# A hybrid RWKV-7 / gMLP layer in one launch: split weights kept two pieces ahead through the last product, with a fourth buffer, and its operand loads issued by ScalarE

## The chip, the cores and the metric

The kernel runs on one core of one Trainium2 chip. The metric is the device time of one execution in microseconds. The time before is the median of three runs, 3248.74 us (3248.45 to 3251.41). A separate execution of the same program was recorded by the hardware profiler; all traces below come from it.

## What is computed

One inference step of one layer, on 512 latent tokens and 128 context tokens (T = 640) of width 2048, all in float32. The reference, cut to the layer:

```python
h = _rmsnorm(x, lp['norm1_g']) * (1.0 + sc1) + sh1
p = h @ lp['w_in']
o_a, s_fin = _rwkv7_bidir(shift_fn(p[..., :C_SHIFT], lp['mu_shift']), s0, lp)
o_b = _chunk_gmlp(jax.nn.gelu(p[..., C_SHIFT:]), lp)
x = x + g1 * (jnp.concatenate([o_a, o_b], axis=-1) @ lp['w_out'])
h = _rmsnorm(x, lp['norm2_g']) * (1.0 + sc2) + sh2
ff = (jax.nn.silu(h @ lp['w_ffn_gate']) * (h @ lp['w_ffn_up'])) @ lp['w_ffn_down']
return x + g2 * ff, s_fin
```

A last RMS norm follows. The part of interest is the last product, with w_ffn_down: 5632 hidden values to 2048 columns.

## The kernel before

**One float32 product as three.** TensorE works on a rounded format (the type fp32r in the profile). A float32 matrix is split into a high part (a rounding copy) and a low part (what the copy left out), and a product is the sum of high x high, high x low and low x high: three matmuls for each block of 128 hidden values (a k-block), at L1817, L1818 and L1819. Weights are split when they arrive, by `parts`: ScalarE copies the high part (L1635), VectorE subtracts the low part (L1636). Each pair hi, lo takes a buffer until its matmuls are done.

**Seven products instead of eight.** The product is cut into two halves of tokens (320 each), two of columns and two of hidden values, and `seven` makes it with seven block products instead of eight, in the order PORD = 1, 2, 3, 7, 5, 6, 4. Each product multiplies one piece of weights: a loaded block (b11, b21, b22), or a difference that GpSimd (POOL) makes from them (`combined`, L1730; the tile t3 and the overwritten blocks b12, b22, b21; a difference shows as `t<-rawd` or `rawd<-rawd`). The activations must be in seven corresponding forms. In the gate phase before, the forms 3, 5 and 4 are split and stored as ready halves in d_os; 1, 2, 7 and 6 are stored whole in d_op.

**The last phase.** The 22 pairs of hidden blocks are cut into six chunks c of 3, 3, 4, 4, 4 and 4 k-blocks (CHK), and each chunk walks over eight column pairs n: 48 steps, seven products each. A product is 9 matmuls of 128x320 in the first two chunks, 12 in the others. A step's results are added to `acc` in SBUF (L2034, L2036, L2038); the first chunk writes it. In the last step of a chunk (a turn) the results stay in PSUM banks for the next chunk's first step. In the last chunk the banks start with acc (`filled`, ScalarE copies at L2116), and each step ends with row work: residual, transposes back to tokens on TensorE (L2097), copies and sums of squares on ScalarE (L2098, L2101).

**What sets the order.** In `seven` the program splits one piece ahead of the product that runs: `ready` holds as many pieces at the start as b11 has blocks, in this phase one, and each product appends the next. The splits of a step begin in that step. A scheduler then places the instructions of each engine in an order of its own; TensorE's stays the program's. `parts` takes its buffers from `st`, three of them; in the gate phase each fourth split uses a buffer of the pool `gu`, which `gus` names. Before the last phase `gus` is emptied and `gu` is closed, so there are three.

**Operands of a chunk.** While a turn runs, `load_ops` fetches the next chunk's operands: `direct` loads the split forms from d_os into their place (`xd`, L1856); `load` fetches the whole forms from d_op into four rotating buffers (`opd`, L1862), and `part` splits them: ScalarE casts (L1869), VectorE subtracts (L1870), GpSimd for some k. All these loads, the weights' (L1841), and the gate phase's stores to d_os (L1940) are issued by SyncE (SP) in one order, and an issue waits in that queue until its buffer is free.

**At the border into the phase.** The last gate block's product 4 is added (L1974), passed through silu (L1975), multiplied (L1976); GpSimd makes its sums (L1919, L1921, L1924); `part` splits and stores them: cast `sp` on ScalarE (L1937), subtraction (L1938), stores (L1940). Then the pool `dn` is opened on the closed pools' space.

Of the kernel before, what the change touches and what calls it, by code (L numbers as in the profile page):

```python
# [54 lines left out]
CHK = (3, 3, 4, 4, 4, 4)  # L55
# [263 lines left out]
def flow_step(ctx: ExitStack, tc, x_prompt, x_sample, state_rwkv, c, c_ctx, w_mod, b_mod,  # L319
# [3 lines left out]
    nc = tc.nc  # L323
# [23 lines left out]
    for h in range(2):  # L347
        s = slice(CH * h, CH * h + CH)
# [29 lines left out]
    d_op = dp.tile([NFF // 2, 7, P, HALF], F32, name="d_op")  # L378
# [10 lines left out]
    st = ctx.enter_context(tc.tile_pool(name="st", bufs=3, side="right"))  # L389
# [754 lines left out]
    parts, praw = {}, []  # L1144
# [150 lines left out]
    with ExitStack() as ph:  # L1295
# [17 lines left out]
        for k in (1, 3):  # L1313
            s = slice(32 * k, 32 * k + 32)
# [265 lines left out]
    def xpool(i, j):  # L1580
        return xep if i < 3 and j < 4 else xcp if j < 4 else xdp
# [33 lines left out]
    PW, READY, gus = [], [], []  # L1615
# [13 lines left out]
    turn4 = itertools.cycle(range(4))  # L1629

    def parts(raw, nk=4):
        pool, kw = (gus[0], dict(bufs=1)) if gus and next(turn4) == 3 else (st, {})
        hi = pool.tile([P, 4, P], F32R, tag="hi", name="hi", **kw)
        lo = pool.tile([P, 4, P], F32R, tag="lo", name="lo", **kw)
        S.copy(hi[:, 0:nk], raw[:, 0:nk])  # L1635
        V.tensor_sub(lo[:, 0:nk], raw[:, 0:nk], hi[:, 0:nk].bitcast(F32))  # L1636
        return hi, lo

    with ExitStack() as ph:
# [21 lines left out]
        for hf in range(2):  # L1661
            s = slice(HALF * hf, HALF * hf + HALF)
            for m in range(KB):
                pool = pbig if m % 2 == 0 else pb2
# [20 lines left out]
        for _ in range(2):  # L1685
            READY.append(parts(PW.pop(0)))
# [36 lines left out]
    def tick():  # L1723

        while len(hooks) > lag[0]:
            hooks.pop(0)()

    def combined(out, a, b, nk=4):
        for o, p, q in zip(out, a, b):
            G.tensor_tensor(out=o[:, 0:nk], in0=p[:, 0:nk], in1=q[:, 0:nk], op=ALU.subtract)  # L1730
# [61 lines left out]
    def fresh(i):  # L1792

        return pP.tile([P, 512], F32, tag="P", name=f"P{i}")[:, 0:HALF], False

    def seven(b11, b12, b21, b22, x, hook, nk=4, bank=fresh, last=True):

        def combine(out, a, b):
            combined(out, a, b, nk)
        t3 = [st.tile([P, 4, P], F32, tag="raw", name="t3", bufs=3) for _ in b11]  # L1800
        combine(t3, b22, b12)
        combine(b12, b12, b11)
        src = {1: b11, 2: b21, 3: b22, 7: t3, 5: b12, 6: b22, 4: b21}
        order = [raw for i in PORD for raw in src[i]]

        ready = [parts(order.pop(0), nk) for _ in range(len(b11))]
        for o, i in enumerate(PORD):
            ps, filled = bank(i)
            nq = len(b11)
            for q in range(nq):  # L1810
                hi, lo = ready.pop(0)
                if order:
                    ready.append(parts(order.pop(0), nk))
                for k in range(nk):
                    xk = x(i, 4 * q + k)
                    f, l = q == 0 and k == 0 and not filled, q == nq - 1 and k == nk - 1 and last
                    TE.matmul(ps, hi[:, k, :], xk[:, 0, :], start=f, stop=False)  # L1817
                    TE.matmul(ps, hi[:, k, :], xk[:, 1, :], start=False, stop=False)  # L1818
                    TE.matmul(ps, lo[:, k, :], xk[:, 0, :], start=False, stop=l)  # L1819
            if i == 3:  # L1820
                combine(b22, b22, b12)
                combine(b21, b21, b22)
            if last:
                hooks.append(lambda o=o, ps=ps: hook(o, ps))
            tick()
            yield o
# [3 lines left out]
    starts = [sum(CHK[:c]) for c in range(len(CHK))]  # L1830

    steps = [(c, n) for c in range(len(CHK)) for n in (range(8) if c % 2 == 0 else range(7, -1, -1))]
    WD, XD = {}, {}

    def load_down(s):
        if s < len(steps):
            c, n = steps[s]
            for b, r, m in (("11", 0, 0), ("21", 1, 0), ("22", 1, 1), ("12", 0, 1)):
                raw = xap.tile([P, 4, P], F32, tag=next(wtags), name="rawd")
                r0 = (starts[c] + r * NFF // 2) * P  # L1840
                nc.sync.dma_start(raw[:, 0:CHK[c], :], w_ffn_down[  # L1841
                    0, r0:r0 + CHK[c] * P, (2 * n + m) * P:(2 * n + m + 1) * P].rearrange("(k p) n -> p k n", p=P))
                WD[s, b] = raw
                yield
# [3 lines left out]
    def load_ops(c):  # L1848

        got = {}  # L1850
        new = lambda i, k: xpool(i, k).tile([P, 2, HALF], F32R, tag=f"xo{i}_{k}", name="xd")

        def direct(i):
            for k in range(CHK[c]):
                XD[i, k] = x = new(i, k)
                nc.sync.dma_start(x.bitcast(F32), d_os[starts[c] + k, SPLIT.index(i)])  # L1856

        def load(i):
            for k in range(0, CHK[c], 2):
                n = min(2, CHK[c] - k)  # L1860
                t = xap.tile([P, 2, HALF], F32, tag=next(stags), name="opd")
                nc.sync.dma_start(t[:, 0:n, :], d_op[starts[c] + k:starts[c] + k + n, i - 1].rearrange("k p t -> p k t"))  # L1862
                got.setdefault(i, []).append((k, n, t))

        def part(i):
            for k, n, t in got[i]:
                for q in range(n):
                    XD[i, k + q] = x = new(i, k + q)
                    S.copy(x[:, 0, :], t[:, q, :])  # L1869
                    (G if (k + q) in POOLK else V).tensor_tensor(out=x[:, 1, :], in0=t[:, q, :],  # L1870
                                                               in1=x[:, 0, :].bitcast(F32), op=ALU.subtract)
        load(1)
        load(2)
        yield
        part(1)
        load(7)
        yield
        part(2)
        direct(3)
        load(6)  # L1880
        yield
        part(7)
        yield
        direct(5)
        part(6)
        yield
        direct(4)
        yield
# [96 lines left out]
    for f in range(2, NFF):  # L1985
        b = {n: [WB.pop((f, n, q)) for q in range(2)] for n in ("11", "12", "21", "22")}
# [24 lines left out]


    dn = ctx.enter_context(tc.tile_pool(name="dn", bufs=1))
    acc = dn.tile([P, 8, 7 * HALF], F32, name="acc")
    sse = dn.tile([P, NT, 8], F32, name="sse")
    slot = lambda n, i: acc[:, n, (i - 1) * HALF:i * HALF]
# [25 lines left out]
    def load_x1(n):  # L2042
        if n >= 0:
            xqs[n] = [xap.tile([P, T], F32, tag=f"x1_{(1, 9)[m]}", name="x1d") for m in range(2)]
            for m in range(2):
                nc.sync.dma_start(xqs[n][m], d_x1[2 * n + m])
# [62 lines left out]
    def filled(n, i):  # L2109
        k = fill.index((n, i))  # L2110
        for m, j in fill[k:k + 2]:
            if (m, j) not in banks:
                banks[m, j] = ps = fresh(j)[0]
                x = XD[1, 0][:, 0, :]
                TE.matmul(ps, x[:, 0:P], x, start=True, stop=False)
                S.copy(ps, slot(m, j))  # L2116
        return banks[n, i], True

    held = {}
    for s, (c, n) in enumerate(steps):  # L2120
        b11, b21, b22, b12 = ([WD.pop((s, b))] for b in ("11", "21", "22", "12"))
        dloads = itertools.chain(dloads, load_down(s + 2))
        final, turn, after = c == NC - 1, s % 8 == 7 and c < NC - 1, s % 8 == 0 and c > 0
        if final or turn and c == NC - 2:
            bank = lambda i, n=n: filled(n, i)
        elif after:
            bank = lambda i: (held[i], True)
        elif turn:
            def bank(i):
                held[i], _ = fresh(i)  # L2130
                return held[i], False
        else:
            bank = fresh
        if c >= NC - 2 and (final or turn):
            lag[0] = LAST_LAG
        for o in seven(b11, b12, b21, b22, lambda i, k: XD[i, k], None if turn else Last(n) if final else Sum(n),
                       CHK[c], bank, not turn):
            if turn:
                if o == 1:
                    ops = load_ops(c + 1)  # L2140
                    next(ops)
                if o in AT:
                    next(ops)
            elif s % 8 == 0 and o in BT:
                next(ops)
            if o > 2:
                next(dloads, None)
            if final and after and o == 2:
                load_x1(n)
            while later and o >= later[0][0]:  # L2150
                later.pop(0)[1]()
            if s == len(steps) - 1 and o == 5:
                while hooks:
                    hooks.pop(0)()
# [52 lines left out]
```

## Time and profile before

| | us |
|---|---|
| median of three runs | 3248.74 |
| profiled execution | 3247.45 |
| its span, from first to last instruction | 3244.2 |
| TensorE matmuls busy | 3107.5 |
| VectorE busy | 2333.3 |
| ScalarE busy | 1446.0 |
| GpSimd busy | 1260.9 |

The granted TensorE clock of the execution was 0.983 on average. In the rows of the profile PE is TensorE, PEld its weight loads, DVE VectorE, ACT ScalarE, POOL GpSimd, SP SyncE; a q behind a name is the engine's sequencer, which issues the DMAs. A row of a timeline gives start, length, engine, line, operation, output and inputs by their names in the program, and in brackets the idle time ahead and what ended it. A row of the waits names an engine and line, what it waited for, and total us, count and longest. A matmul's length overlaps the next one's; what counts is the distance from start to start.

### The profile page before, as it was taken

The page shows a single profiled execution, that of the slowest core. Times are in us where ns is not written, and L with a number is a line of the kernel's source. Part 1 is how long each engine was busy: PE and PEld are TensorE (multiplying, and loading weights), DVE is VectorE, ACT ScalarE, POOL GpSimd, SP SyncE. Part 2 cuts the span into 40 slices and gives each one's busy share as a digit, 9 for nine tenths or more (in the row PEclk, how much of TensorE's full clock was granted, in tenths as well). Part 3 has the DMA queues.
Part 4 walks back from the last instruction along what each step waited for, and adds up shares of the span by engine and source line. Part 5 has one row for each costly group of instructions (what it writes and reads, how often), then busy time and mean ns, then how long its engine had stood idle before and what let it go on. Part 6 is the DMA issues. An engine that isn't in the chain of part 4 may idle for free. (4 is left out here: it accounts for less than half of the span.)

```text
span 3244.2 us, 73519 instructions
## 1 busy us (share of the span) xinstructions
PE 3107.5 (96%) x28828; PEld 2877.5 (89%) x28828; DVE 2333.3 (72%) x4073; ACT 1446.0 (45%) x3161; POOL 1260.9 (39%) x1082
## 2 busy tenths in 40 slices
PE   5899999999998999898999999999999999999996
PEld 3698888889886877788999999999999999999986
DVE  4456767767666666547977877877877777777787
ACT  3244554555543333345644444444444444444365
POOL 0001222222220122301365666566666645555543
PEclk8899999999997999999999999999999999999998
DMA  8768788887896777455434434434433354554353
GB/s 319 254 183 237 212 224 212 237 233 192 230 233 191 215 222 226 136 152 175 123 108 130 125 105 128 127 107 123 123 116 118 110 180 151 160 160 141 110 170 119
DMA packets 741922, 553.00 MB, mean 170 GB/s; under 512 B 141688, under 2 KB 674184, under 8 KB 732744
## 3 DMA queue, kind: packets, MB, share of 16 engines
q1 hardware_dynamic: 729256, 534.62, 55.5%
q0 software_dynamic: 9984, 13.13, 1.7%
q8 instruction: 226, 3.70, 0.5%
q14 instruction: 120, 0.98, 0.1%
q10 hardware_dynamic: 2336, 0.57, 0.1%
HBM read 438.77 MB, written 111.69 MB: 170 GB/s over the span
## 5 line engine op out<-in xcount | busy, mean ns | idle before, releaser
L1819 PE MATMUL P<-xo,lo 128*128 128x320 f32 x2352 | 727.1, 309 | 3.5 <-DVE lo L1636 3.5
L1818 PE MATMUL P<-xo,hi 128*128 128x320 f32 x2352 | 727.6, 309 | 0.0
L1817 PE MATMUL P<-xo,hi 128*128 128x320 f32 x2352 | 727.6, 309 | 0.0
L1636 DVE TENSOR_TENSOR lo<-raw,hi 128x512 fp32r<-128x512 f32 x532 | 514.4, 974 | 162.0 <-ACT hi L1635 159.6
L1635 ACT CAST hi<-raw 128x512 fp32r<-128x512 f32 x532 | 330.2, 622 | 505.6 <-PE P L1818 435.6
L1819 PEld LDWEIGHTS P<-xo,lo 128*128 128x128 f32 x2352 | 441.6, 188 | 4.3 <-DVE lo L1636 4.2
L1818 PEld LDWEIGHTS P<-xo,hi 128*128 128x128 f32 x2352 | 442.3, 188 | 0.0
L1817 PEld LDWEIGHTS P<-xo,hi 128*128 128x128 f32 x2352 | 442.3, 188 | 0.0
L1730 POOL TENSOR_TENSOR raw<-raw 128x512 f32<-128x512 f32 x252 | 413.6, 1645 | 13.6 <-DVE lo L1636 0.6
L106 PE MATMUL big<-h_hi,hi 128*128 128x320 f32 x1280 | 417.8, 326 | 0.9 <-ACT praw L1209 0.9
L1819 PE MATMUL P<-xd,lo 128*128 128x320 f32 x1232 | 384.4, 312 | 16.8 <-DVE lo L1636 16.2
L106 PE MATMUL big<-h_lo,hi 128*128 128x320 f32 x1280 | 394.1, 308 | 0.0
L106 PE MATMUL big<-h_hi,lo 128*128 128x320 f32 x1280 | 394.1, 308 | 0.0
L1817 PE MATMUL P<-xd,hi 128*128 128x320 f32 x1232 | 381.9, 310 | 5.1 <-ACT hi L1635 3.0
L1818 PE MATMUL P<-xd,hi 128*128 128x320 f32 x1232 | 380.7, 309 | 0.0
L1730 POOL TENSOR_TENSOR t<-raw 128x512 f32<-128x512 f32 x84 | 129.5, 1542 | 454.8 <-DMA raw<-in_w_ffn_up_dram 407.5
L1635 ACT CAST hi<-rawd 128x512 fp32r<-128x512 f32 (+1 forms) x288 | 168.7, 588 | 237.9 <-PE P L1818 198.5
L106 PEld LDWEIGHTS big<-h_hi,hi 128*128 128x128 f32 x1280 | 240.7, 188 | 32.6 <-issue 25.9
L1819 PEld LDWEIGHTS P<-xd,lo 128*128 128x128 f32 x1232 | 231.2, 188 | 25.6 <-DVE lo L1636 25.6
L106 PEld LDWEIGHTS big<-h_lo,hi 128*128 128x128 f32 x1280 | 240.7, 188 | 1.2
L106 PEld LDWEIGHTS big<-h_hi,lo 128*128 128x128 f32 x1280 | 240.1, 188 | 0.0
L1817 PEld LDWEIGHTS P<-xd,hi 128*128 128x128 f32 x1232 | 231.4, 188 | 8.6 <-ACT P L2116 4.8
(370 smaller groups left out, 6268.3 us busy)
## 6 DMA issues: line engine op xcount, KB each, us to landing
wt<-in_w_mod_dram SPq DMA_DIRECT2D x96, 1024.0 KB
raw<-in_w_ffn_gate_dram SPq DMA_DIRECT2D x182, 256.0 KB
raw<-in_w_ffn_up_dram SPq DMA_DIRECT2D x182, 256.0 KB
rec<-d_S SPq DMA_DIRECT2D x80, 576.0 KB
raw<-in_w_in_dram SPq DMA_DIRECT2D x172, 256.0 KB
rawd<-in_w_ffn_down_dram SPq DMA_DIRECT2D x128, 256.0 KB
raw<-in_w_out_dram SPq DMA_DIRECT2D x96, 256.0 KB
xd<-d_os SPq DMA_DIRECT2D x66, 320.0 KB
```

Of the source, the lines that this page charges most:

```text
L106: self.eng, self.run = eng, lambda: fn(*args, **kw)
L1635: S.copy(hi[:, 0:nk], raw[:, 0:nk])
L1636: V.tensor_sub(lo[:, 0:nk], raw[:, 0:nk], hi[:, 0:nk].bitcast(F32))
L1730: G.tensor_tensor(out=o[:, 0:nk], in0=p[:, 0:nk], in1=q[:, 0:nk], op=ALU.subtract)
L1817: TE.matmul(ps, hi[:, k, :], xk[:, 0, :], start=f, stop=False)
L1818: TE.matmul(ps, hi[:, k, :], xk[:, 1, :], start=False, stop=False)
L1819: TE.matmul(ps, lo[:, k, :], xk[:, 0, :], start=False, stop=l)
```

## The change

Three edits. First, `parts` takes each fourth buffer from the pool that `gus` names last, and `gus` names `dn` in the last phase: four buffers there instead of three. Second, `seven` starts with two pieces ready, and while the last two products of a step run it splits the first two pieces (b11, b21) of the next step, into the list `ahead`, so that splits go on across the border of steps and chunks. Third, the loads of opd are issued by ScalarE's queue.

```diff
@@ parts
-        pool, kw = (gus[0], dict(bufs=1)) if gus and next(turn4) == 3 else (st, {})
+        pool, kw = (gus[-1], dict(bufs=1)) if gus and next(turn4) == 3 else (st, {})
@@ seven
+    ahead = []
+
-    def seven(b11, b12, b21, b22, x, hook, nk=4, bank=fresh, last=True):
+    def seven(b11, b12, b21, b22, x, hook, nk=4, bank=fresh, last=True, then=()):
...
-        ready = [parts(order.pop(0), nk) for _ in range(len(b11))]
+        order, ready = order[len(ahead):], ahead[:]
+        ahead.clear()
+        while len(ready) < 2:
+            ready.append(parts(order.pop(0), nk))
+        then = list(then)
...
                 if order:
                     ready.append(parts(order.pop(0), nk))
+                elif then:
+                    step = then.pop(0)
+                    ahead.append(parts(WD[step], CHK[steps[step[0]][0]]))
@@ load_ops, load
-                nc.sync.dma_start(t[:, 0:n, :], d_op[starts[c] + k:starts[c] + k + n, i - 1].rearrange("k p t -> p k t"))
+                nc.scalar.dma_start(t[:, 0:n, :], d_op[starts[c] + k:starts[c] + k + n, i - 1].rearrange("k p t -> p k t"))
@@ the last phase
     dn = ctx.enter_context(tc.tile_pool(name="dn", bufs=1))
+    gus.append(dn)
...
+        then = [(s + 1, b) for b in ("11", "21")] if s + 1 < len(steps) else ()
         for o in seven(b11, b12, b21, b22, lambda i, k: XD[i, k], None if turn else Last(n) if final else Sum(n),
-                       CHK[c], bank, not turn):
+                       CHK[c], bank, not turn, then):
```

Lines below the first edit move down by up to ten: L1870 becomes L1879, L1940 becomes L1949, L2116 becomes L2126.

**The start of the phase, ScalarE.** First the order before, then the order of the change, from the second copy of step 0 on. The names: hi is the high part of a weight piece, sp the cast of a last gate operand; the numbers are tile numbers. In brackets stands what an instruction waits for, by engine or by DMA lane. Before, hi_33374 is the second piece of step 0 (its source is rawd_33283):

```order
L1635 CAST hi_33374<-rawd_33283 128x384 [waits DMAHW3_49,DVE_49,PE_49]
L1635 CAST hi_33403<-rawd_33319 128x384 [waits DVE_49,PE_49]
L1975 ACTIVATE c_33279<-c_33279 128x640 [waits DVE_49]
L1635 CAST hi_33423<-t3_33366 128x384 [waits PE_49,Activation_49,Pool_49]
L1937 CAST sp_33344<-act_33325 128x320 [waits DVE_49]
L1635 CAST hi_33439<-rawd_33321 128x384 [waits PE_49,Activation_49,Pool_49]
L1937 CAST sp_33349<-act_33089 128x320 [waits Pool_49]
```

After the change the same piece, now hi_33373, stands here:

```order
L1635 CAST hi_33427<-rawd_33321 128x384 [waits PE_49,Pool_49]
L1878 CAST xd_33397<-opd_33240 128x320 [waits DMAHW7_49]
L1946 CAST sp_33344<-act_33325 128x320 [waits DVE_49]
L1946 CAST sp_33349<-act_33089 128x320 [waits Pool_49]
L1878 CAST xd_33400<-opd_33240 128x320
L1878 CAST xd_33403<-opd_33242 128x320 [waits DMAHW2_49]
L1871 DMA opd_34252<-d_op_90 128x2x320 [waits DVE_49]
L1946 CAST sp_33354<-act_33325 128x320 [waits Pool_49]
L1871 DMA opd_34254<-d_op_90 128x320 [waits DMAHW3_49,DVE_49]
L1635 CAST hi_33373<-rawd_33283 128x384 [waits DMAHW4_49,DMAHW5_49,DMAHW1_49,DMAHW6_49,DMAHW0_49,DVE_49]
```

The second piece's copy moved behind the copies of pieces three to five and behind the last of the three casts sp; its buffer is the new one in dn, and the lanes it waits for are those of the stores of the sp tiles, among others.

**A turn, VectorE.** The place is the step in which the operands of the fourth chunk are split; xd are the operands' low parts, lo those of the weights, t the combination that is the step's fourth piece. Before:

```order
L1636 TENSOR_TENSOR lo_36400<-rawd_36336,hi_36399 128x512
L1870 TENSOR_TENSOR xd_36442<-opd_36415,xd_36442 128x320
L1870 TENSOR_TENSOR xd_36445<-opd_36415,xd_36445 128x320
L1870 TENSOR_TENSOR xd_36448<-opd_36417,xd_36448 128x320
L1636 TENSOR_TENSOR lo_36425<-t3_36374,hi_36424 128x512
L1870 TENSOR_TENSOR xd_36494<-opd_36419,xd_36494 128x320
```

After the change:

```order
L1636 TENSOR_TENSOR lo_36387<-rawd_36340,hi_36386 128x512
L2048 TENSOR_TENSOR acc_33364<-acc_33364,P4_36362 128x320
L1636 TENSOR_TENSOR lo_36404<-t3_36382,hi_36403 128x512
L1879 TENSOR_TENSOR xd_36446<-opd_36419,xd_36446 128x320
L1879 TENSOR_TENSOR xd_36449<-opd_36419,xd_36449 128x320
L1879 TENSOR_TENSOR xd_36452<-opd_36421,xd_36452 128x320
L1636 TENSOR_TENSOR lo_36429<-rawd_36360,hi_36428 128x512
```

The split of t moved ahead of the three operand subtractions.

**The same turn, ScalarE after the change.** The loads of opd now stand in its order, and an issue waits there until VectorE and GpSimd have used the buffer's old contents:

```order
L1635 CAST hi_36403<-t3_36382 128x512 [waits DVE_49,PE_49]
L1878 CAST xd_36446<-opd_36419 128x320 [waits PE_49]
L1878 CAST xd_36449<-opd_36419 128x320 [waits PE_49]
L1878 CAST xd_36452<-opd_36421 128x320 [waits PE_49]
L1635 CAST hi_36428<-rawd_36360 128x512 [waits DVE_49,PE_49]
L1878 CAST xd_36455<-opd_36421 128x320 [waits PE_49]
L1871 DMA opd_36458<-d_op_90 128x2x320 [waits DMAHW4_49,DVE_49]
L1871 DMA opd_36460<-d_op_90 128x2x320 [waits DMAHW6_49,DVE_49,Pool_49]
L1635 CAST hi_36463<-rawd_36340 128x512 [waits PE_49]
```

Before, the two DMA rows stood in SP's order. The high part of the next but one piece, hi_36463, is now queued behind them.

## The prediction

> **What bounds the kernel now.** I read the page's busy shares first: TensorE (PE) is busy 96% of the span, so only time in which PE stands still can be won. The change touches the last phase only, the w_ffn_down product from 2625 us on, so I cut that phase into windows. A row gives the window, its length, and for each engine the busy time with the number of instructions; PEclk is the granted TensorE clock.
>
> ```profile
> core 0: us, PE busy (x) PEld busy (x) DVE busy (x) ACT busy (x) POOL busy (x), PEclk, DMA share, GB/s
> 2625.00:2640.00 15.00, 11.25 (x68) 9.71 (x67) 11.97 (x20) 8.52 (x21) 7.03 (x7) 1.00 0.70 234
> 2640.00:2661.00 21.00, 19.99 (x133) 19.18 (x132) 13.58 (x28) 9.59 (x23) 10.18 (x9) 1.00 0.67 200
> 2690.00:2730.00 40.00, 37.32 (x248) 36.01 (x247) 29.89 (x53) 20.46 (x47) 19.98 (x18) 1.00 0.66 206
> 2778.00:2794.00 16.00, 12.88 (x84) 11.86 (x82) 13.84 (x22) 8.44 (x19) 7.21 (x7) 1.00 0.76 268
> 2794.00:2880.00 86.00, 86.00 (x587) 86.00 (x587) 60.62 (x99) 32.76 (x56) 48.75 (x30) 1.00 0.40 114
> 2880.00:2896.00 16.00, 13.82 (x90) 12.87 (x89) 13.36 (x21) 7.91 (x16) 7.01 (x7) 1.00 0.92 320
> 2979.00:2998.00 19.00, 16.70 (x110) 15.74 (x109) 16.34 (x23) 10.17 (x22) 10.21 (x8) 1.00 0.80 277
> 3078.00:3100.00 22.00, 20.20 (x133) 19.14 (x132) 16.73 (x24) 14.88 (x35) 11.55 (x9) 1.00 0.68 235
> 3112.00:3218.00 106.00, 100.87 (x676) 96.09 (x675) 89.24 (x136) 69.19 (x196) 37.72 (x25) 1.00 0.32 95
> ```
>
> The row 2794:2880 is the inside of a chunk: 587 matmuls in 86.00 us, gapless, 0.1465 us each. So a piece of weights (9 matmuls in the chunks of three k-blocks, 12 in those of four) keeps PE busy for 1.32 or 1.76 us, and inside a chunk nothing can be won: a fourth buffer is worth nothing there. Length minus matmuls x 0.1465 is what PE lost elsewhere: at the start 15.00 - 9.96 = 5.04 and 21.00 - 19.48 = 1.52; at the five turns from chunk to chunk 40.00 - 36.33 = 3.67, then 3.69, 2.81, 2.88 and 2.52; in the last chunk 106.00 - 99.03 = 6.97. In all 29.1 us. The waits say who ended them:
>
> ```profile
> PE P L1819 <- DVE lo L1636: 16.2, 22, 1.8
> PE P L1817 <- ACT hi L1635: 3.0, 3, 1.6
> ACT hi L1635 <- PE P L1818: 231.3, 231, 2.7
> ACT xd L1869 <- DMA opd<-d_op: 27.6, 14, 3.7
> ```
>
> That is total us, times, longest, in 2625 to 3218. PE waits for the low part of a weight piece, made by DVE, almost alone. The third row is no bottleneck by itself: ScalarE's high-part copies wait for PE to give a buffer back, once for most pieces, because there are three buffers and each is still being multiplied. It shows how short the lead is. The stall at one turn, chunk 2 to 3, in DVE's timeline, SP's timeline and the chain of waits (start us, length us):
>
> ```profile
> 2877.05 3.49 DVE L1870 TENSOR_TENSOR xd<-opd,xd 128x320 fp32r<-128x320 f32 x3
> 2880.46 1.34 DVE L1636 TENSOR_TENSOR lo<-t,hi 128x512 fp32r<-128x512 f32 x1
> ```
> ```profile
> 2881.74 1.84 SPq L1856 DMA_DIRECT2D xd<-d_os  x4
> 2883.68 0.90 SPq L1862 DMA_DIRECT2D opd<-d_op  x2
> 2884.79 6.91 SPq L1856 DMA_DIRECT2D xd<-d_os  x8
> ```
> ```profile
> 2881.86 0.43 PE P L1819
> ...
> 2883.68 6.74 DMA opd<-d_op
> 2890.44 0.47 ACT xd L1869
> ...
> 2892.71 0.96 DVE lo L1636
> 2893.72 0.41 PE P L1819
> ```
>
> Two causes. First, three operand subtractions (3.49 us) stand ahead of the low part of the piece that PE takes next, so PE starts at 2881.86 what it could have had at 2880.3. Second, an operand pair takes 6.74 us to land, because four xd loads went into the same queue just before it; behind its cast stand the splits of the next pieces, and PE waits again at 2893.72.
>
> **The change, part by part.** The number of splits, subtractions, matmuls and bytes stays the same; only order, buffers and the issuing queue change.
>
> (a) *The fourth buffer and two pieces ahead, at the turns.* In the changed order the low part of that piece stands ahead of the three subtractions, so it comes 3.49 us sooner, against a wait of 1.4 us: this stall goes. What is late next are the subtractions, put back by the 1.34 us of one split; the lead across the border is two pieces, 2 x 1.76 = 3.52 us, which covers that. By the same reading each turn keeps a little: I leave 1.0 at the first (a lead of 2 x 1.32 only), 0.5, 0.3 and 0.4 at the next three, 0.8 at the last, where bank fills on ScalarE also end waits. Gain 15.57 - 3.0 = 12.6. Bounds: 0 (DVE is 13.84 busy of 16.00 us at the second turn, so order alone might buy nothing) to 15.6.
>
> (b) *The last chunk.* There the row work of each step (transposes, sums, bank fills) stands on ScalarE and DVE ahead of the second piece's split; in the changed order that split stands ahead. The waits of PE in 3112 to 3218:
>
> ```profile
> PE P L1819 <- DVE lo L1636: 3.9, 7, 0.8
> ```
>
> Each wait costs PE about 0.16 more than its idle time (at 2881.86 start to start was 1.72, idle 1.41), so 3.9 + 7 x 0.16 = 5.0 us could go. ScalarE is 69 busy of 106, DVE 89, so there is room. I take 4.0, bounds 0 to 5.0.
>
> (c) *Operand loads on ScalarE's queue.* No wait for a DMA issue of ScalarE shows in this phase; the nearest price is the program's first issue there:
>
> ```profile
> L453 ACTq DMA_DIRECT2D crow<-in_c_dram x1: 425/425/425, 0.7 to 0.7; - x1
> ```
>
> A chunk's eight loads at 0.425 are 3.4 us, set into turns in which ScalarE is busy 8 of 16 us: hidden, cost 0, while the lead of two pieces holds; without that lead up to 3.4 per turn. What the issue waits for is the matter of the first rival.
>
> By **DMA: Bandwidth & Descriptors** of the Trainium skill, Issuing engines are not separate DMA queues, this part should bring only the issue time; by its section Queues, rings and completion order the engines take turns between the two queues' rows, so a pair on the second queue would pass the xd backlog. The row of 6.74 us is from a single queue and decides neither; the first would leave the second stall of each turn, the third rival.
>
> (d) *The start of the phase* loses. The new fourth buffer lies in the pool dn, opened on space of the gate phase. The first split that uses it is the second piece of step 0, and in the changed program its copy waits for the landing of the last stores of the gate phase's operand halves, d_os<-sp: they read from that space. PE takes its pieces in order, so it stands still until then. Those stores in the kernel before:
>
> ```profile
> 2627.66 0.41 PE L1817 MATMUL P<-xd,hi 128*128 128x320 f32 x1 [0.85 <-ACT hi L1635]
> 2629.48 1.50 DVE L1976 TENSOR_TENSOR act<-act,c 128x640 f32<-128x640 f32 x1 [0.34 <-ACT c L1975]
> 2629.28 2.56 POOL L1730 TENSOR_TENSOR rawd<-rawd 128x384 f32<-128x384 f32 x2 [8.27 <-DVE lo L1636]
> 2634.32 1.07 POOL L1924 TENSOR_TENSOR act<-act 128x320 f32<-128x320 f32 x1
> 2635.42 0.46 ACT L1937 CAST sp<-act 128x320 fp32r<-128x320 f32 x1 [0.45 <-POOL act L1924]
> 2636.67 0.48 SPq L1940 DMA_DIRECT2D d_os<-sp  x1
> 2639.26 1.08 ACT L2034 COPY acc<-P 128x320 f32<-128x320 f32 x3
> ```
>
> The eviction at 2639.26, into the same pool with the same wait, started 2.59 us after the last store's issue: taken as its landing. There the wait hurt nobody, since PE had free banks. In the changed order POOL has one combination (half of 2.56) fewer ahead of the chain, the sum L1974 stands a split (0.5) earlier on DVE, and no weight load stands ahead of the last store: together some 2.5 us, so a landing near 2636.7, and with half a microsecond each for high and low part PE goes on at about 2637.5. Ends: 2635.5 if everything in the chain also runs faster, 2640.0 if it moves nowhere. Without waits PE would take that piece at 2627.66 - 0.85 - 0.16 = 2626.65, so the loss is 10.85; what was lost there before (5.04 + 1.52) goes, as pieces 2 to 4 are split meanwhile. Net +4.3, from +2.3 to +6.8.
>
> A standstill of some 10 us also costs clock. The trace of before shows it elsewhere:
>
> ```profile
> 1539.68 0.42 PE L1749 MATMUL C<-xo,hi 128*128 128x320 f32 x1 [2.51 <-ACT hi L1635]
> ```
> ```profile
> 1541.50:1544.50 3.00, 3.00 (x13) 3.00 (x13) 2.17 (x5) 1.95 (x6) 0.00 (x0) 0.50 0.65 183
> ```
>
> After an idle of 2.51 us and some broken work the clock was 0.50 for 3 us: 13 matmuls where 3.00 / 0.1465 = 20.5 fit, 7.5 x 0.1465 = 1.1 us lost, with its edges 1.5. I add 1.5 (bounds 0 and 3). **TensorE: Matmul & The Clock Gate** of the Trainium skill, Part 1, gives half rate after an idle window of about 3.4 us and until a busy one; this case's trace shows the half rate after less idle time, and the sum is by the trace.
>
> **Sum.** -12.6 - 4.0 + 4.3 + 1.5 = -10.8 us against the profiled execution (3247.45, of which 3244.2 is the span): 3236.7. The median of the runs shown lies 1.3 above that execution, so 3238 by it; I forecast 3237.
>
> **Rivals.**
>
> *ScalarE's queue becomes the blocker (slower).* An operand load waits until DVE and POOL have used the buffer's old contents. On SP that wait stood here:
>
> ```profile
> SPq L1862 <- DVE xd L1870: 38.8, 13, 6.2
> ```
>
> Now ScalarE itself waits, in order, and behind it stand the high-part copies, behind them DVE's low parts, behind them PE. Of a mean wait of 3.0 us, one piece of lead (1.5) is covered if the second piece is already used up by the subtractions; 38.8 - 13 x 1.5 = 19.3 us then reach PE, the turns' old losses stay, the last chunk gains 4.0, the start loses 5.8: 3247.45 + 21.1 = 3268.5. It decides where ScalarE is held for longer than the split pieces last, 2.64 or 3.52 us. For it: the longest wait of 6.2. Against it: in the changed order one or two high-part copies stand ahead of each such load, and the subtractions it waits for are issued right before. Chance 0.15.
>
> *DVE is the bound at the turns (no change).* With DVE 13.84 of 16.00 busy and subtractions that take 1.2 us each in 2877 to 2880, moving them only moves the stall: half of (a), 6.3, and 1 of (b), against 5.8 lost: 3247.45 - 1.5 = 3246. For it: DVE is the engine that PE waits for. Against it: in the windows inside chunks DVE is 60.6 busy of 86, so a backlog of one or two splits is caught up. Chance 0.22.
>
> *The loads land as late as now.* The second stall of each turn (at this one idle until 2893.72) stays, about 0.6 a turn: +3, 3240. Chance 0.15.
>
> *The start does not wait* (the change does not do there what I read): -16.6, and the old start losses in part gone, -4: 3227. Chance 0.06.
>
> *The forecast*, within 3231 to 3243: 0.42.
>
> **Range and chances.** A measurement of this kernel tells from no change what differs by about 0.2%, 6.5 us: faster means under 3242.2, slower over 3255.2. Faster: 0.42 + 0.15 + 0.06 less 0.03 for the forecast's upper edge, 0.60; same 0.25; slower 0.15. The range leaves out the first rival and the far ends: low with the start's lost time at its least and all of (a) and (b), 3247.45 - 20.6 + 2.3 = 3229, and further to the start that does not wait, 3226; high with (a) and (b) at nearly nothing and the start at its worst, 3247.45 - 3 + 9 = 3254.
>
> **What would show it.** Right: one idle time of PE of some 9 us just behind the phase's first nine matmuls, ended by a high-part copy or a low part at about 2637, then a stretch at clock 0.5; windows at the turns with under 1 us lost; PE's waits for the low part in the last chunk nearly gone. Wrong: waits of PE at the turns ended by high-part copies, with ScalarE held ahead of them by a DMA issue (first rival); turn windows that lose 2 us and more with DVE nearly full (second); operand loads that still take 5 to 7 us (third); no gap at the start (fourth).

## The result and the profile after

| | before | after |
|---|---|---|
| median of five runs, us | 3250.66 | 3273.06 |
| lowest to highest | 3248.45 to 3257.39 | 3271.82 to 3275.10 |
| profiled execution (span) | 3247.45 (3244.2) | 3275.1 (3273.3) |

The change makes the kernel slower: the ratio is 1.0068 (95% interval 1.0053 to 1.0082). 3237 was forecast, within 3226 to 3254.

The windows of the changed kernel, cut at the places where it lost time (columns as in the prediction; the phase begins some 3 us later in this execution):

```profile
core 0: us, PE busy (x) PEld busy (x) DVE busy (x) ACT busy (x) POOL busy (x), PEclk, DMA share, GB/s
2629.00:2650.00 21.00, 4.43 (x21) 3.55 (x20) 13.02 (x21) 6.98 (x16) 7.25 (x7) 0.61 0.73 244
2650.00:2655.00 5.00, 5.00 (x24) 5.00 (x23) 1.51 (x3) 1.45 (x4) 0.00 (x0) 0.60 0.14 39
2723.50:2739.00 15.50, 11.33 (x66) 10.81 (x65) 9.37 (x17) 7.18 (x18) 4.44 (x5) 0.89 1.01 335
2804.80:2825.40 20.60, 15.82 (x87) 14.89 (x86) 13.74 (x21) 8.26 (x17) 8.28 (x6) 0.83 0.95 301
2911.60:2931.00 19.40, 15.57 (x86) 14.90 (x85) 12.63 (x21) 7.68 (x17) 7.16 (x6) 0.82 1.07 344
2931.00:3004.00 73.00, 73.00 (x500) 73.00 (x499) 51.95 (x84) 26.00 (x42) 38.06 (x25) 1.00 0.31 90
3017.20:3035.00 17.80, 14.22 (x86) 13.57 (x85) 13.57 (x21) 7.48 (x16) 7.52 (x6) 0.90 1.06 348
3109.00:3140.00 31.00, 29.15 (x184) 28.25 (x184) 21.26 (x34) 17.86 (x41) 14.41 (x12) 0.94 0.76 255
3140.00:3246.70 106.70, 102.71 (x706) 100.53 (x706) 84.99 (x140) 70.38 (x199) 36.40 (x26) 1.00 0.35 97
```

Length minus matmuls x 0.1465, as before: the start loses 17.92 + 1.48 = 19.4 us (6.6 before), the five turns 5.83, 7.85, 6.80, 5.20 and 4.04, together 29.7 (15.6 before), the last chunk 3.3 (7.0 before). Start +12.8, turns +14.1, last chunk -3.7: together +23.2 us, where the medians differ by 22.4. Inside a chunk PE is gapless as before (73.00 of 73.00). At the first four turns the DMA share is at or near 1 (0.76 at the fifth), and PEclk is under 1 in the window of the start and in those of the five turns.

The waits of PE from 2610 us to the end of the phase, us in total, times, longest:

```profile
PE P L1826 <- ACT hi L1635: 17.1, 6, 4.2
PE P L1826 <- DMA rawd<-in_w_ffn_down_dram: 15.9, 1, 15.9
...
PE P L1828 <- DVE lo L1636: 1.9, 6, 0.5
```

The many short waits for VectorE's low parts (16.2 us in 22) are nearly gone. In their place stand few long ones: one of 15.9 us at the start, one of 3.5 to 4.2 us at each of the first four turns and one of 1.1 us at the fifth, those at the turns ended by ScalarE's high-part copy.

**The start.** Timelines of ScalarE, VectorE, SP and PE. `c` at L1983 is the last gate block's sum, the head of the chain that ends in the stores to d_os:

```profile
2631.57 0.82 ACT L1878 CAST xd<-opd 128x320 fp32r<-128x320 f32 x2 [1.68 <-DMA opd<-d_op]
2634.44 0.48 DVE L1983 TENSOR_TENSOR c<-P,pq 128x320 f32<-128x320 f32 x1
2643.18 0.38 ACTq L1871 DMA_DIRECT2D opd<-d_op  x1
2643.60 0.46 ACT L1946 CAST sp<-act 128x320 fp32r<-128x320 f32 x1 [3.28 <-DVE xd L1879]
2644.08 0.32 SPq L1949 DMA_DIRECT2D d_os<-sp  x1
2647.51 0.51 ACT L1635 CAST hi<-rawd 128x384 fp32r<-128x384 f32 x1 [3.45 <-DMA d_os<-act]
2648.07 0.64 PE L1826 MATMUL P<-xd,hi 128*128 128x320 f32 x1 [15.86 <-DMA rawd<-in_w_ffn_down_dram]
```

PE's row names a weight load, but that was long there; what came last is the row above it, the copy that waited for the gate phase's stores. This is the wait that the prediction saw. It came later than forecast because the chain's head came late (ScalarE stood on operand loads that it had issued itself) and because the third cast `sp` stood 3.28 us behind one more issue, the one at 2643.18, which waited until VectorE had subtracted a pair (`xd` at L1879).

**A turn,** chunk 2 to 3. Timelines of ScalarE, SP and PE:

```profile
2908.26 2.81 ACTq L1871 DMA_DIRECT2D opd<-d_op  x2
2911.12 0.62 ACT L1635 CAST hi<-rawd 128x512 fp32r<-128x512 f32 x1 [2.59 <-PE P L1828]
...
2917.01 0.82 ACT L1878 CAST xd<-opd 128x320 fp32r<-128x320 f32 x2 [3.30 <-DMA opd<-d_op]
2919.41 0.46 ACT L1878 CAST xd<-opd 128x320 fp32r<-128x320 f32 x1 [1.59 <-DMA opd<-d_op]
...
2920.13 0.61 ACT L1635 CAST hi<-t 128x512 fp32r<-128x512 f32 x1
```
```profile
2905.99 13.78 SPq L1865 DMA_DIRECT2D xd<-d_os  x12
```
```profile
2920.80 0.64 PE L1826 MATMUL P<-xd,hi 128*128 128x320 f32 x1 [3.76 <-ACT hi L1635]
...
2922.47 0.47 PE L1827 MATMUL P<-xd,hi 128*128 128x320 f32 x1
2922.74 0.47 PE L1828 MATMUL P<-xd,lo 128*128 128x320 f32 x1
```

The turn's own step no longer stops. The stop has moved to the fourth product of the next step: the copy of its piece (`hi<-t`) stands on ScalarE behind casts of two operand pairs. They were issued at 2908.26 and 2910.71 (one row here) and are used only at 2917.01 and 2919.41, 8.75 and 8.70 us later (6.74 before). SP issues its twelve xd loads in one row beside them. The packets of the two queues, q1 of SP and q10 of ScalarE, with their number, MB and share of the 16 DMA engines, first from 2908.3 to 2912, then from 2912 to 2915:

```profile
q1 hardware_dynamic: 740, 1.17, 98.7%
```
```profile
q1 hardware_dynamic: 354, 0.81, 69.8%
q10 hardware_dynamic: 302, 0.37, 34.1%
```

ScalarE's queue moves nothing until 2912.17, 3.9 us after the first pair's issue, while SP's packets run; an opd load issued at 2904.50, with no transfer of SP's under way, had its first packet 1.0 us after the issue. From 2912 on the two queues take turns, nearly packet for packet, but ScalarE's packets carry half as much, so SP's loads get two thirds of the bytes. PE's stop costs twice: 3.76 us idle, and afterwards matmuls 0.267 us apart instead of 0.1465.

### The profile page after: what moved, and what is told of

It reads as the page before. It is cut to its first block, busy times and chain, and to the rows that moved or that the text cites. A ratio compares the mean times of both kernels' runs of the same rounds, so it can differ in the third digit from the quotient of the medians.

```text
span 3273.3 us, 73510 instructions
## 1 busy us (share of the span) xinstructions
PE 3117.3 (95%) x28828; PEld 2889.9 (88%) x28828; DVE 2310.5 (71%) x4073; ACT 1445.2 (44%) x3161; POOL 1247.6 (38%) x1082
## 3 DMA queue, kind: packets, MB, share of 16 engines
q1 hardware_dynamic: 717224, 520.20, 53.6%
## 5 line engine op out<-in xcount | busy, mean ns | idle before, releaser
L1826 PE MATMUL P<-xd,hi 128*128 128x320 f32 x1232 | 387.5, 315 | 34.3 <-ACT hi L1635 17.1
L1827 PE MATMUL P<-xd,hi 128*128 128x320 f32 x1232 | 385.5, 313 | 0.0
L106 PEld LDWEIGHTS big<-h_hi,hi 128*128 128x128 f32 x1280 | 241.0, 188 | 33.5 <-issue 26.7
L1636 DVE TENSOR_TENSOR lo<-rawd,hi 128x512 fp32r<-128x512 f32 (+1 forms) x288 | 211.0, 738 | 56.6 <-ACT hi L1635 47.5
```

What stands on the lines that cost most here:

```text
L106: self.eng, self.run = eng, lambda: fn(*args, **kw)
```

## The experiments

In the table below stand all kernels; each edit and its expectation follow. "Lost" is what PE lost, from the first matmul of a group of steps to that of the next, less the gapless time (0.1467 us a matmul; 12.3 us of a last-chunk step), in one profiled execution each: at the start (the end of the gate phase's last product and steps 0 to 6), around the five turns (steps 7 to 40) and in the last chunk (steps 41 to 47, transposes included). The phase begins between 2623.4 and 2637.3 us in these executions, so the times do not follow the sums to the us.

| kernel | median us | ratio to before (95%) | start | turns | last | sum |
|---|---|---|---|---|---|---|
| before | 3249.6 to 3251.4 | | 7.2 | 18.7 | 24.7 | 50.5 |
| the change | 3273.06 | 1.0068 (1.0053 to 1.0082) | 20.9 | 34.3 | 20.8 | 75.9 |
| opd_on_sp | 3248.20 | 0.9991 (0.9980 to 1.0001) | 14.6 | 12.1 | 21.7 | 48.3 |
| queue_only | 3269.94 | 1.0050 (1.0034 to 1.0066) | 14.3 | 38.0 | 23.2 | 75.5 |
| three_buffers | 3265.71 | 1.0043 (1.0029 to 1.0057) | 14.4 | 29.0 | 25.7 | 69.1 |
| late_dn_sp | 3242.95 | 0.9971 (0.9960 to 0.9983) | 8.7 | 12.8 | 22.4 | 43.8 |
| part6_kept | 3272.26 | 1.0075 (1.0058 to 1.0092) | 18.2 | 30.5 | 25.0 | 73.7 |
| six_opd | 3271.15 | 1.0072 (1.0057 to 1.0087) | 20.5 | 26.7 | 23.2 | 70.3 |
| three_buffers_sp | 3251.18 | 1.0001 (0.9991 to 1.0011) | 7.8 | 19.6 | 26.3 | 53.6 |
| best2 | 3239.33 | 0.9969 (0.9955 to 0.9982) | 8.5 | 10.7 | 23.0 | 42.1 |
| late_76_act | 3259.26 | 1.0032 (1.0016 to 1.0049) | 10.7 | 30.6 | 20.8 | 62.0 |
| late_12_act | 3259.54 | 1.0031 (1.0017 to 1.0045) | 14.1 | 24.2 | 23.3 | 61.5 |
| no_border | 3238.12 | 0.9964 (0.9951 to 0.9977) | 6.5 | 12.9 | 21.5 | 40.9 |
| best3 | 3242.27 | 0.9979 (0.9968 to 0.9989) | 8.4 | 9.2 | 23.7 | 41.3 |
| no_xd | 3271.45 | 1.0063 (1.0051 to 1.0076) | 20.7 | 25.6 | 19.7 | 66.0 |
| fourth_only | 3236.83 | 0.9956 (0.9943 to 0.9969) | 6.1 | 11.0 | 22.2 | 39.3 |
| best4 | 3236.52 | 0.9959 (0.9947 to 0.9970) | 6.5 | 8.5 | 22.8 | 37.8 |

**opd_on_sp: the change with the queue edit undone**

```diff
-                nc.scalar.dma_start(t[:, 0:n, :], d_op[starts[c] + k:starts[c] + k + n, i - 1].rearrange("k p t -> p k t"))
+                nc.sync.dma_start(t[:, 0:n, :], d_op[starts[c] + k:starts[c] + k + n, i - 1].rearrange("k p t -> p k t"))
```

> The change with one edit undone: the opd loads are issued by SyncE again; the fourth buffer in dn and the two pieces ahead stay. Theory Q (ScalarE's queue is the main loss: it issues the operand loads late and is held ahead of the weight copies): the gate phase's last sum is back at about 2628 us, the second piece of step 0 still waits for the stores into dn's space and starts at 2637 to 2640 instead of 2648; the stop of some 4 us at the fourth product of each chunk's first step goes. Against before: +6 at the start, -8 at the turns, -4 in the last chunk, about 3245 us. Theory O (the order of two pieces ahead is the loss, because the casts of the last operand pair now stand ahead of the fourth piece's copy): the stops at the turns stay, 5 to 7 us each, and the time is above 3260.

Measured 3248.2, 3 us above the expectation and not to be told from before: the turns fall from 34.3 to 12.1, under before's 18.7, and the start from 20.9 to 14.6. Theory Q holds. The wait for dn's space is left by itself at the start, in the timelines of ScalarE and PE:

```profile
2643.48 0.51 ACT L1635 CAST hi<-rawd 128x384 fp32r<-128x384 f32 x1 [3.06 <-DMA d_os<-sp]
```
```profile
2644.05 0.63 PE L1826 MATMUL P<-xd,hi 128*128 128x320 f32 x1 [12.25 <-DMA rawd<-in_w_ffn_down_dram]
```

Counted from the gate phase's last product, the phase begins 5.0 us later here than before, so this is 2639.1 in the time of before's trace; the change's 2648.07, 3.4 later in the same way, is 2644.7.

**queue_only: the kernel before with the queue edit alone** (the line above, the other way round)

> The kernel before with this one edit: the opd loads are issued by ScalarE. Three buffers, one piece ahead, no splits across borders. Theory Q: the gate phase's last sum comes some 6 us late as in the change, and each turn stops for 3 us and more: slower than before by 15 to 25 us, about 3270. Theory O: the queue by itself costs only its issue time, 3250 within 4 us.

Measured 3269.9, as theory Q had it: most of the loss of the change comes from the one line. With the phase's later begin taken off, the gate phase's last sum comes 3 us late, as in the change, not 6. PE's waits in this phase:

```profile
PE P L1819 <- DVE lo L1636: 15.7, 19, 3.2
PE P L1817 <- ACT hi L1635: 14.7, 12, 3.6
```

**three_buffers: the change without its fourth buffer**

```diff
-    gus.append(dn)
```

> The change without its fourth buffer (dn is not handed to the splits); opd on ScalarE's queue and two pieces ahead stay. Theory B (the wait for the landing of the last gate stores is paid because the second piece's buffer lies in dn): the standstill of 16 us at step 0 shrinks to a few us, 3273 - 11 = 3262, and the turns stop as in the change. Rival (the start is lost to the late sum alone): the standstill stays above 10 us and the time within 3 us of the change's 3273.

3265.7, between the two expectations. The standstill goes, as theory B had it (stops of 3.81 and 2.79 us are left), but the start's loss falls only by 6.5, to 14.4: ScalarE's copies still stand behind casts that wait for an operand load, 3.21 us in the longest case. With opd_on_sp above and three_buffers_sp below the start is a sum: 7.8 with neither the buffer nor the queue, 6.6 to 6.8 more with either of them (14.4, 14.6), 20.9 with both.

**late_dn_sp: opd on SyncE, dn handed out from step 2 on**

```diff
-    gus.append(dn)
...
+        if s == 2:
+            gus.append(dn)
```

> The change with opd back on SyncE's queue and dn handed to the splits only from step 2 on. Theories Q and B together: no wait at the start, turns and last chunk gain as forecast for the change (8 to 12 and 4 us): 3236 to 3240 us, faster than both kernels. Theory O: the turns stop for 5 us and more, 3255 or above.

3243.0, faster than both kernels, 3 to 7 us short of the expectation: the turns gain 5.9 and the last chunk 2.3.

**part6_kept: the change, with form 6's casts behind the fourth product**

```diff
-                    S.copy(x[:, 0, :], t[:, q, :])
+                    cast = S.copy(x[:, 0, :], t[:, q, :])
+                    if i == 6:
+                        tc.keep_in_program_order(cast)
...
         direct(5)
-        part(6)
         yield
         direct(4)
         yield
+        part(6)
+        yield
...
-    AT, BT = (2, 4, 6), (0, 1)
+    AT, BT = (2, 4, 6), (0, 1, 3)
```

> The change, with one move: in the first step of a chunk the casts of the last whole operand (form 6, used by the step's sixth product) are written behind the fourth product and kept there in ScalarE's order, so that the copies of the fourth to sixth weight pieces stand ahead of them. Theory C (those casts wait for loads that land late, and the fourth piece's copy is held behind them): the stops of some 4 us at the fourth product, and the clock that they cost, go: the turns lose 15 instead of 34 us, 3255 us. Rival L (the loads are too late for the products themselves): the stop moves to the sixth product and stays, 3268 or more.

3272.3, not theory C's 3255 but what rival L had: the turns still lose 30.5. The stops at the fourth product went, and others took their place at the sixth: in the same step at the first two turns, ended by form 6's cast (1.5 us) and by its subtraction on GpSimd (3.5 us), and one step later at the next two, ended by high-part copies (1.9 and 3.4 us).

**six_opd: the change with six opd buffers**

```diff
-tags(8, 1, 0, 9), tags(6, 7, 0, 8)
+tags(8, 1, 0, 9, 6, 7), tags(6, 7, 0, 8)
```

> The change with six rotating buffers for opd instead of four (two more tags of the same size), so that an issue on ScalarE's queue seldom waits for VectorE and GpSimd. Theory W (the issue's wait on ScalarE is what costs at the turns): ScalarE's idle times ahead of DMA issues go, the turns lose 20 to 25 instead of 34 us, 3260. Theory C: the loads of the last pair still land late behind the backlog of xd loads, the stops at the fourth product stay, 3273 within 5 us.

3271.2. In the profile the turns lose 7.6 less, in the time nothing clear comes of it. Neither theory fits. After the first four turns the stops at the fourth product are gone, but PE stops for 2.0 to 2.7 us at the sixth product one step later. At the turn from chunk 2 to 3 the copy of that piece waits for GpSimd's combination, and GpSimd stood 9.14 and 2.37 us for weight blocks that landed late. Nor did the two buffers take the wait of the issues away: ScalarE's idle time just ahead of its opd issues, added up from 2640 us on, is 26.6 us in the change and 31.0 here. So this run doesn't price that wait.

**three_buffers_sp: two pieces ahead and border splits alone** (opd_on_sp and three_buffers together)

> Only the second edit: two pieces ahead and splits across the borders; opd on SyncE, three buffers, dn not used. If the fourth buffer is worth something at the turns and in the last chunk, this is slower than the same kernel with it from step 2 on (3243): 3247 to 3250. If two pieces of lead with three buffers do as well: 3243 within 3 us.

3251.2, ratio 1.0001: without the fourth buffer the second edit gains nothing, in none of the three places.

**best2: late_dn_sp with form 6's casts kept as in part6_kept**

> opd on SyncE, two pieces ahead, the fourth buffer from step 2 on, and the casts of form 6 kept behind the fourth product's split as in the first of these runs. By theory C the turns lose 6 instead of 13 us: 3243 - 6 = 3237, faster than both kernels. By rival L no gain over 3243.

3239.3; its interval and that of late_dn_sp overlap. The turns lose 10.7 instead of 12.8: the move that failed with the loads on ScalarE is worth some 2 us in the profile with them on SyncE.

**late_76_act and late_12_act: late_dn_sp with half of the opd loads on ScalarE**

```diff
-                nc.sync.dma_start(t[:, 0:n, :], d_op[starts[c] + k:starts[c] + k + n, i - 1].rearrange("k p t -> p k t"))
+                (nc.scalar if i in (7, 6) else nc.sync).dma_start(t[:, 0:n, :], d_op[starts[c] + k:starts[c] + k + n, i - 1].rearrange("k p t -> p k t"))
```

In late_12_act the condition is `i in (1, 2)`.

> The kernel of late_dn_sp (opd on SyncE, fourth buffer from step 2 on, 3243 us) with the loads of forms 7 and 6 alone moved to ScalarE's queue: the four loads that are issued and needed within a turn. If these are what costs at the turns (issued late, behind the xd loads that SyncE now sends ahead of them), the turns lose 25 us and more instead of 13, and the start a few: 3255 to 3262. If the prefetches of forms 1 and 2 are what costs, 3245.

> The same kernel with the loads of forms 1 and 2 alone on ScalarE's queue: the prefetches for the next chunk, which there pass the weight loads that SyncE sends first. If these cost at the turns (weights land late), the turns lose 20 us and more, 3252 or above. If forms 7 and 6 are what costs, within 4 us of 3243.

3259.3 and 3259.5: each half by itself costs 16 us over late_dn_sp, both together 25 (the change against opd_on_sp). The first half makes the stop at the fourth product. The second makes others, a part of them at the start (14.1 lost instead of 8.7, the wait of 5.5 us among it): PE's waits in late_12_act are

```profile
PE P L1826 <- ACT hi L1635: 8.0, 5, 5.5
PE P L1828 <- DVE lo L1636: 6.7, 10, 2.7
PE P L1826 <- DMA xd<-d_os: 5.0, 7, 2.4
```

The last row does not appear among the waits before: xd loads are now late, though nothing about them was changed but what runs beside them.

**no_border: late_dn_sp without splits across the border**

```diff
-        then = [(s + 1, b) for b in ("11", "21")] if s + 1 < len(steps) else ()
+        then = ()
```

> The kernel of late_dn_sp without splits across the border of steps: each step starts by splitting its first two pieces itself. If the fourth buffer alone carries the gain, 3243 within 3 us. If the border splits carry it, the gain goes: 3250.

3238.1, 2 us under the first expectation. Nothing is lost without the border splits.

**best3: best2 with form 6's loads ahead of form 3's**

```diff
         part(2)
-        direct(3)
         load(6)
+        direct(3)
```

> The kernel of best2 (3239) with the loads of form 6 put ahead of form 3's xd loads in SyncE's queue at each turn. If loads land in the order of their issue, this pair lands some 3 us after its issue instead of 6.5, and form 3's loads 1.7 us later than before; with the casts already behind the fourth product nothing waited for the pair, so the time is 3239 within 4 us. If form 3 becomes late for the third product of the next step, 3245 or more.

3242.3, not to be told from best2. Since the casts are kept back, the time of the casts doesn't show when the pair landed.

**no_xd: the change without the xd loads after the first chunk**

```diff
             for k in range(CHK[c]):
+                if (i, k) in XD:
+                    continue
                 XD[i, k] = x = new(i, k)
```

> The change, but from the second chunk on the split operands of forms 3, 5 and 4 are not loaded again (the first chunk's stay in place, so part of the product is computed with the wrong operands; matmuls, splits and the order on ScalarE stay). Theory D (the opd pair lands late because it stands in line behind the xd loads, whichever queue issued it): the pair lands some 3 us after its issue instead of 8.7, the stops at the fourth product go, the turns lose 8 to 14 instead of 34 us: 3249 to 3253. Theory W (ScalarE is held by the wait of the issue itself): the stops stay, the turns lose 25 and more, 3264 or above.

3271.5: the turns lose 25.6, 8.7 less, but not the 8 to 14 of theory D; loss and time are those of theory W, though the stop isn't, as the timelines show. The kernel leaves out all xd loads after the first chunk but those of the fourth k-block, which chunk 2 loads for the first time. The turn from chunk 2 to 3 in the timelines of ScalarE, VectorE and PE:

```profile
2907.33 1.72 ACTq L1873 DMA_DIRECT2D opd<-d_op  x2
...
2912.27 0.82 ACT L1880 CAST xd<-opd 128x320 fp32r<-128x320 f32 x2 [0.58 <-DMA opd<-d_op]
...
2914.14 0.62 ACT L1635 CAST hi<-t 128x512 fp32r<-128x512 f32 x1
```
```profile
2912.76 4.09 DVE L1881 TENSOR_TENSOR xd<-opd,xd 128x320 fp32r<-128x320 f32 x3 [0.35 <-ACT xd L1880]
...
2917.17 1.35 DVE L1636 TENSOR_TENSOR lo<-t,hi 128x512 fp32r<-128x512 f32 x1
```
```profile
2918.57 0.41 PE L1828 MATMUL P<-xd,lo 128*128 128x320 f32 x1 [2.22 <-DVE lo L1636]
```

With the xd loads gone the pair is used 4.94 us after its issue instead of 8.75, and the copy `hi<-t` is in time. Now VectorE's subtractions of the same pair, 4.09 us for three while GpSimd works beside them, hold the low part. So the late landing is a cause of the stop at the fourth product, and at this turn the next in line takes over most of what it frees.

**fourth_only: the kernel before, with the fourth buffer from step 2 on**

```diff
-        pool, kw = (gus[0], dict(bufs=1)) if gus and next(turn4) == 3 else (st, {})
+        pool, kw = (gus[-1], dict(bufs=1)) if gus and next(turn4) == 3 else (st, {})
...
+        if s == 2:
+            gus.append(dn)
```

> The kernel before with a fourth buffer in dn from step 2 on and nothing else (one piece ahead, no splits across borders, opd on SyncE). If the buffer alone carries the gain of the kernels with opd on SyncE: 3238 to 3243. If it needs the second piece ahead within the step: 3250 within 3 us.

3236.8: 0.44% faster than before (0.31% to 0.57%), and as fast as the best of those with a second piece ahead. The buffer carries the gain. Its waits in this phase, of PE and of ScalarE:

```profile
PE P L1819 <- DVE lo L1636: 7.3, 12, 1.1
ACT hi L1635 <- PE P L1818: 164.2, 167, 2.2
```

Before they were 16.2 in 22 and 231.3 in 231: with a fourth buffer a copy need not wait for PE as often, so the split is early by itself, whatever the program writes as the lead.

**best4: no_border with form 6's casts kept as in best2**

> The kernel of no_border (3238) with the casts of form 6 kept behind the fourth product, as in best2. If both gains add: 3235; if the casts' place matters only with border splits: 3238 within 3 us. Faster than before by 0.3% either way.

3236.5. It adds nothing that can be told from fourth_only.

## Why the prediction was wrong

- **What bounds the kernel: right.** Time was won and lost only at the start, at the turns and in the last chunk.
- **(c), the queue, is the step that failed.** The prediction said of the eight issues a chunk: "hidden, cost 0, while the lead of two pieces holds". Put alone on the kernel before, they cost 0.50% (3269.9), and taken from the change they give back 25 us. What was priced was the length of an issue, 0.425 us. What was not: in SP's order the opd loads had a place, behind some xd loads and ahead of others, and the prefetches behind the weights; on ScalarE they are issued when ScalarE gets there, and SP's loads are ahead of them by then (the first packet left 3.9 us after the issue at the turn shown). Then their landing delays casts, and the casts delay copies, in ScalarE's order: 8.75 us from issue to use, and 3.76 us of standstill.
- **(a), the turns:** -12.6 forecast, +14 measured. With the queue edit undone they gain 6.6, half the forecast. The lead across the border was named as the cover; no_border and three_buffers_sp show that it covers nothing, and fourth_only that the buffer does it. "A fourth buffer is worth nothing there" was right for the inside of chunks and kept me from pricing it by itself at the turns.
- **(b), the last chunk: right in size,** -4.0 forecast, -3.7 by the windows. The reason (the second piece's split ahead of the row work) isn't borne out: with three buffers and two pieces ahead the chunk loses 26.3 against 24.7, with the buffer alone 22.2. So the size came out by luck; the losses are those of single executions.
- **(d), the start: right in mechanism, mis-sized in the change.** PE was to go on at 2637.5, at the latest at 2640.0. That was reckoned from the last d_os<-sp store of before (2636.67); its timeline has a d_os<-act store after it, and in the change the copy's wait is ended by such a one. With the loads on SP PE goes on at 2639.1, and the net loss is 14.6 - 7.2 = 7.4 us against 5.8 forecast, clock included. With them on ScalarE it is 2644.7: the sum at the chain's head comes 2.6 us later than in opd_on_sp, the way from it to the last store takes 9.64 instead of 7.21, the landing 0.6 more. This term also had to be worked out with the queue edit in place, and was not.
- **The first rival** (3268.5) had the sign, the size and the engine. Its mechanism, an issue that holds ScalarE, is seen at the start (3.28 us ahead of the third cast `sp`) and between the two issues of the turn (2908.26 to 2910.71); what it costs by itself isn't shown, since six_opd did not shorten ScalarE's idle time ahead of its issues. The other part is the one in the third rival, loads that land no earlier, which I had priced at +3.
- **The two queues.** The pair on ScalarE's queue is used 8.75 us after its issue beside SP's xd loads, 4.94 us without them. That fits **DMA: Bandwidth & Descriptors** of the Trainium skill, Issuing engines are not separate DMA queues (all run on the same engines). The taking of turns that the prediction named is there too, 302 packets against 354 from 2912 on, but it didn't let the pair pass the backlog: the pair's first packet left 3.9 us after the issue. Why it left so late isn't shown.
- **Open:** how the queue's loss at the turns (38.0 - 18.7 = 19.3 us alone, 34.3 - 12.1 = 22.2 in the change) divides. Removing the xd loads (no_xd) takes 8.7 off in one profile, two more buffers (six_opd) 7.6 and a later place of the casts (part6_kept) 3.8, and none moved the time clearly. They were not tried together, and no run takes the issue's wait away by itself.

## What to carry to other kernels

A DMA issue that moves to another engine's queue moves its wait too, and gives up its place in the order of the loads it left; price the order of landing and what stands behind the first use, not the length of the issue. A change of three edits is to be priced edit by edit and each also with the others in place: here the buffer from step 2 on gives 14 us, the second piece ahead nothing, and the queue takes some 20. And a standstill is not spread evenly: short waits cost their length, long ones can cost the clock after them too.

## What was not expected of the hardware

A stop of 3.76 us at a turn was followed by matmuls 0.267 us apart for about 6 us (the window's clock is 0.82), some 2.9 us more: 6.80 lost in that window less 3.76 and the 0.16 of a restart. The turns before stopped for 1.77 us and less, at a clock of 1.00. So the change, by joining short stops into a long one, nearly doubled its price. The 15.86 us at the start cost no more clock than that (1.48 us in 2650 to 2655, and some in the two us before).

The length of a stop alone doesn't tell what it costs. Just behind a stop of 2.44 us in best2 (first row) and one of 2.22 us in no_xd (second):

```profile
3106.70:3109.70 3.00, 2.94 (x20) 2.94 (x21) 2.70 (x7) 1.84 (x5) 0.00 (x0) 1.00 0.53 159
```
```profile
2918.50:2924.00 5.50, 5.43 (x26) 5.43 (x27) 5.35 (x9) 1.87 (x4) 2.45 (x2) 0.69 0.76 220
```

The longer stop was followed by a clock of 1.00, the shorter by 0.69.
